# Seven-product groups with their weight sums apart from the instructions that read them, and a fifth such group in five blocks of the first feed-forward

## The chip, the core and the metric

One Trainium2 chip, one of its cores. The metric is the device time of one execution in microseconds (us). The kernel before takes 2227.85 us, the median of three runs (2227.22 to 2228.51).

## What is computed

One decoder layer on 256 tokens of width 2048, all in float32: a SwiGLU feed-forward, two parallel mixers (retention and sliding-window attention), a second SwiGLU feed-forward, and a gated input embedding, each closed by a layer norm. The change lies in the products with weights, above all in the first line below for the first feed-forward:

```
D_MODEL = 2048; SEQ = 256; D_FF = 5632

def swiglu(x, w_gu, w_down):
    g, u = jnp.split(x @ w_gu, 2, axis=-1)
    return (jax.nn.silu(g) * u) @ w_down

h = layer_norm(alpha * h + 0.5 * swiglu(h, w_ffn1_gu[i], w_ffn1_down[i]), ...)
```

## The kernel before, in words

**High and low parts.** TensorE multiplies a rounded format, so each float32 operand is cut into a high part and a low part (the rest). A 128x512 product is then three matmuls: low by high, high by high and high by low (lines 459, 460 and 461, in `Sum.add`). A weight chunk of 128x1024 numbers (512 KB) is loaded by SyncE into a tile whose name begins with `r`; ScalarE casts it to the high part, a tile that begins with `h` (line 107); VectorE subtracts that from the chunk and has the low part, a tile that begins with `l` (line 108). ScalarE and VectorE each work through their instructions strictly in the order in which the program wrote them.

**The first feed-forward's gate and up products** (`f1g` and `f1u` in the profile) run in 11 blocks. A block is 512 gate columns and 512 up columns for all 256 tokens, over 16 slices of 128 of the width, taken in 8 pairs. A pair is two chunks, gate (`0_p`, "a" below) and up (`1_p`, "b"). There are three ways to work a pair p off:
- *Plain* (P): ScalarE casts both chunks, VectorE subtracts both; 24 matmuls of TensorE.
- *Folded* (F): the low part of chunk b is made without VectorE. ScalarE writes the negated high part into the low tile (line 170), GpSimd issues a DMA that adds the raw chunk to it (line 171), and ScalarE later casts the high part (line 187). 24 matmuls.
- *Seven* (S, class `Seven`): the two token halves, the two slices, and the two chunks make a 2x2 by 2x2 product, which is done with seven products in place of eight (Winograd's form): 21 matmuls. For it VectorE forms four sums of raw weights, 128x512 each: t1 and t3 lie in one tile (`uf`), t2 and t4 in another (`vf`); t2 reads t3, and t4 reads t2 (lines 256 to 259). Then come the split of chunk a (`hf`, `lf`), of one quarter, b22 (`bf`), of the tile `uf` (`huf`, `luf`) and of `vf` (`hvf`, `lvf`): four casts on ScalarE, four subtractions on VectorE, 128x1024 but for b22. On the token side the same sums are formed once, in block 0 (`forms_sums`, `seven_forms`, `f1fh` and `f1fl`; lines 533 to 536 and 108), for the pairs 0 to 3.

Block 0 is all plain: 192 matmuls. Blocks 1 to 10 run in the order F F S S F S S P, with pairs 0 to 3 as the four S: 180 matmuls each. The units of a block sum into PSUM banks `f1g` and `f1u`, and the groups of seven share four more banks (`f1NsJ` of block N), which are opened anew for each block.

**The end of a block.** In the last S of a block, the seven products run in another order than in the others, so that the banks shared by the groups are complete early. Then follows `seven_common`: ScalarE copies one bank (`eve`, line 578), and VectorE makes four 128x512 sums (lines 579 to 582). I call these the *fold*. After the plain pair that closes the block, VectorE adds the gate banks (line 1085, twice: *G*), the up banks (line 1085, twice: *U*), ScalarE takes the silu (line 1086), and VectorE multiplies (line 1087: *M*). In the next block, the result is turned for the product with `w_down` by ScalarE copies (lines 219 and 226; tiles `wf1`, `mf1` and `f1a`) and a transposing DMA between them.

**What sets the order.** Weights are prepared ahead of their use by a small planner. `fill` makes the next unit in the plan as long as the prepared ones hold less than 45 matmuls and there is room among the 30 tile slots; each unit carries its number of matmuls as `time` and its number of tiles as `makes` and `keeps`. The half of a folded pair is begun 34 matmuls or more ahead (`FOLD_AHEAD`, `fold_at`). All of this is settled when the program is built. So VectorE's order of work is fixed: splits of the units ahead, with the fold, G, U and M between them at the places where the block's own units were used up.

`Seven` also serves the second feed-forward's gate and up products, both products with `w_down`, and two products of the mixers (`w_in`, `w_ret`).

Of the kernel before, what the change touches and what calls it, by code (L numbers as in the profile page):

```python
# [8 lines left out]
F32 = mybir.dt.float32  # L9
F32R = mybir.dt.float32r  # L10
# [3 lines left out]
ALU = mybir.AluOpType  # L14
PSUM = bass.MemoryType.PSUM

P = 128
# [27 lines left out]

AHEAD = {1: (4, 5), 2: (4,), 3: (4, 5), 4: (4,), 5: (4, 5), 6: (4,), 7: (4, 5), 8: (4,)}
AHEAD_SLOTS = 36

DELAY = {"f1": 2, "f2": 1}

# [14 lines left out]
def layer(ctx: ExitStack, tc: tile.TileContext, io):  # L65
# [16 lines left out]
    def slot(shape, dt, name):  # L82
        return slots.tile(shape, dt, tag="slot", name=name)
# [22 lines left out]
    def split(dst_hi, dst_lo, src, lo_engine=None):  # L106
        act.copy(dst_hi, src)  # L107
        (lo_engine or dve).tensor_tensor(dst_lo, src, dst_hi, ALU.subtract)  # L108
# [124 lines left out]
    class Seven:  # L233
# [12 lines left out]
        def make(self):  # L246
            a, b = self.a, self.b
            nm = a.name
            b11, b21, b12, b22 = a.of(a.raw, 0), a.of(a.raw, 1), b.of(b.raw, 0), b.of(b.raw, 1)
            u, v = (slot([P, 2, 512], F32, w + nm) for w in "uv")  # L250

            def shaped(x):
                return x.rearrange("p (g n) -> p g n", g=2) if a.paired else x

            t1, t3, t2, t4 = (shaped(x) for x in (u[:, 0], u[:, 1], v[:, 0], v[:, 1]))
            dve.tensor_tensor(t1, b11, b12, ALU.add)
            dve.tensor_tensor(t3, b12, b22, ALU.add)  # L257
            dve.tensor_tensor(t2, b11, t3, ALU.add)
            dve.tensor_tensor(t4, t2, b21, ALU.add)  # L259

            def parted(name, x):
                hi, lo = (slot([P, 2, 512], F32R, w + name + nm) for w in "hl")
                split(hi, lo, x)
                return [(hi[:, e], lo[:, e]) for e in range(2)]

            a.make()
            self.b11, self.b21 = a.columns(0), a.columns(1)
            both = slot([P, 2, 512], F32R, "b" + nm)
            self.b22 = both[:, 0], both[:, 1]
            split(shaped(both[:, 0]), shaped(both[:, 1]), b22)  # L270
            self.t1, self.t3 = parted("u", u)
            self.t2, self.t4 = parted("v", v)

    put_by_sums = {}

# [250 lines left out]
    def forms_sums(full):  # L526


        a11, a21 = (full[:, 0::2, t * P : (t + 1) * P] for t in range(2))
        a12, a22 = (full[:, 1::2, t * P : (t + 1) * P] for t in range(2))  # L530
        raw = slot([P, 8, P], F32, "sums")
        f5, f6, f7, f3 = (raw[:, 2 * j : 2 * j + 2, :] for j in range(4))
        dve.tensor_tensor(f5, a21, a22, ALU.subtract)
        dve.tensor_tensor(f7, a11, a21, ALU.subtract)
        dve.tensor_tensor(f6, f5, a11, ALU.subtract)
        dve.tensor_tensor(f3, a12, f6, ALU.add)
        return raw

    def forms_split(raw, hi, lo):

        split(hi, lo, raw)
        return lambda e: [(hi[:, 2 * j + e, :], lo[:, 2 * j + e, :]) for j in range(4)]

    def seven_forms(full, hi, lo, between=None):

# [17 lines left out]
    def units_of(order, sevens, ahead=()):  # L563

        sevens, ahead = list(sevens), list(ahead)
        plain = [p for p in range(KD // 2) if p not in sevens + ahead]
        of = {"S": sevens, "D": ahead, "P": plain, "F": plain}
        return [(kind, of[kind].pop(0)) for kind in order]
# [397 lines left out]
    def gu_units(name, j):  # L966
        if j == 0:
            return [("P", p) for p in range(KD // 2)]
        if name == "f2" and j in AHEAD:
            plain = "P" if j < 4 else "F"  # L970
            return units_of(*((f"P{plain}SDSDSP", SEVEN[:3]) if j % 2 else (f"P{plain}SSDSSP", SEVEN)), AHEAD[j])
        order = "FFSSFSSP" if name == "f1" or j > 8 else "PFSSFSSP"
        return units_of(order, SEVEN[: order.count("S")])

# [28 lines left out]
    def ffn(name, i, ht, norm, keep, residual, keepers, away):  # L1003
# [33 lines left out]
        for j in range(KF // 4):  # L1037
# [22 lines left out]
            def before(u, j=j, offset=KD // 2 - len(units)):  # L1060
                u += offset
                if j == 0 and norm is None and u % 2 == 0:
                    first_chunk(u // 2)
                    if u == 6:
                        slots_for_weights(30)
                    if u == 2:
                        load_constants()
                if j == 0 and u == 7:
                    for g in sorted({p // 2 for p in SEVEN}):
                        hi, lo = (slot([P, 8, P], F32R, f"{name}f{w}{g}") for w in "hl")  # L1070
                        made[g] = seven_forms(keep[g], hi, lo)
# [901 lines left out]
```

## Time and profile before

| what | value |
|---|---|
| median of three runs | 2227.85 us |
| span of the profiled execution | 2226.9 us |
| TensorE busy, matmuls | 2216.5 us, 10137 |
| VectorE busy | 2006.5 us (90%) |
| ScalarE busy | 1440.9 us (65%) |
| TensorE clock granted, mean | 0.999 |
| first feed-forward's gate and up blocks 1 to 10 | from 51.1 to 459.1 us, 40.80 us each |

The answer on the profiled execution gives its span, from the first to the last instruction, and no other time of its own; it is 0.95 us below the median of the runs. An instruction's duration in a timeline includes the tail in which the next one on its engine already starts. What an instruction costs its engine is therefore read as the distance from its start to the start of the next. In a waits list the columns are the total, how often, and the longest. "PEclk" is the granted TensorE clock as a share of full speed.

### The profile page before, as it was taken

To read this page: it belongs to the slowest core of one execution; us is meant where nothing else is said; L and a number is where in the kernel's file an instruction comes from. 1 tells how busy PE (TensorE), PEld (TensorE's weight loads), DVE (VectorE), ACT (ScalarE), POOL (GpSimd) and SP (SyncE) were. 2 spreads that over 40 slices of the span, in tenths; PEclk is the share of its full clock that TensorE was granted. 3 is DMA by queue.
4 is the path that set the end of the run, shared out by engine and by line. 5 is a ranking of instruction groups with operands and counts; after the bars stand their busy time and mean duration, and the time that the engine had idled before them with its cause. 6 is when DMAs were issued, how large, how long until landed. Compare 5 with 4: busy or idle time off the path is not lost.

```text
span 2226.9 us, 29164 instructions
## 1 busy us (share of the span) xinstructions
PE 2216.5 (100%) x10137; PEld 1838.3 (83%) x10137; DVE 2006.5 (90%) x2629; ACT 1440.9 (65%) x1680; POOL 51.7 (2%) x66
## 2 busy tenths in 40 slices
PE   9999999999999999999999999999999999999998
PEld 7888888888888888888788888888888888888887
DVE  6999999999988889789999888779999999999977
ACT  6777777776565545557866567466666677765553
POOL 0000000000000000000000000000000000000000
PEclk9999999999999999999999999999999999999999
DMA  9998998978686889846976568888999988777871
GB/s 310 275 251 251 266 271 233 246 228 256 216 301 239 297 281 336 268 172 228 293 232 236 179 205 319 312 302 270 303 297 298 332 240 270 215 237 240 292 283 68
DMA packets 303917, 576.02 MB, mean 259 GB/s; under 512 B 98829, under 2 KB 103821, under 8 KB 303769
## 3 DMA queue, kind: packets, MB, share of 16 engines
q1 hardware_dynamic: 293576, 541.70, 73.4%
q0 software_dynamic: 8208, 29.89, 7.2%
q10 hardware_dynamic: 1984, 2.58, 0.4%
q8 instruction: 79, 1.29, 0.2%
q14 instruction: 70, 0.57, 0.1%
HBM read 490.20 MB, written 33.55 MB: 235 GB/s over the span
## 4 chain that ended last, share of the span: by engine, by line
PE 94%; DVE 2%; DMA 2%; issue 1%; ACT 0%; SPq 0%; ACTq 0%; DVEq 0%; POOLq 0%
PE f1g L461 3%; PE f1g L459 3%; PE f1g L460 3%; PE rqk L410 3%; PE f1u L461 2%; PE f1u L459 2%; PE f1u L460 2%; PE f2g L461 2%; PE f2g L459 2%; PE f2g L460 2%; PE f2u L461 2%; PE f2u L459 2%; PE f2u L460 2%; PE aqk L410 2%; PE f2e L461 1%; PE f2e L460 1%
## 5 line engine op out<-in xcount | busy, mean ns | idle before, releaser
L108 DVE TENSOR_TENSOR lf_gu<-rf_gu,hf_gu 128x1024 fp32r<-128x1024 f32 (+1 forms) x225 | 268.6, 1210 | 24.9 <-ACT hf_gu L107 24.1
L107 ACT CAST hf_gu<-rf_gu 128x1024 fp32r<-128x1024 f32 (+1 forms) x225 | 229.7, 1039 | 24.7 <-DMA rf_gu<-in_f_gu 24.1
L108 DVE TENSOR_TENSOR lw_in_f<-rw_in_f,hw_in_f 128x1024 fp32r<-128x1024 f32 x140 | 167.9, 1219 | 14.0 <-ACT hw_in_f L107 13.6
L108 DVE TENSOR_TENSOR lf_down<-rf_down,hf_down 128x1024 fp32r<-128x1024 f32 x128 | 153.9, 1220 | 17.3 <-ACT hf_down L107 14.5
L107 ACT CAST hf_down<-rf_down 128x1024 fp32r<-128x1024 f32 x128 | 131.5, 1049 | 41.9 <-DMA rf_down<-in_f_down 15.3
L107 ACT CAST huf_gu<-uf_gu 128x1024 fp32r<-128x1024 f32 x76 | 80.1, 1054 | 113.9 <-DVE uf_gu L257 104.1
L107 ACT CAST hw_in_f<-rw_in_f 128x1024 fp32r<-128x1024 f32 x140 | 140.6, 1048 | 5.9 <-DMA rw_in_f<-in_w_in_f 2.9
L107 ACT CAST hvf_gu<-vf_gu 128x1024 fp32r<-128x1024 f32 x76 | 80.2, 1055 | 32.0 <-DVE vf_gu L259 29.8
L108 DVE TENSOR_TENSOR luf_gu<-uf_gu,huf_gu 128x1024 fp32r<-128x1024 f32 x76 | 92.6, 1218 | 0.0
L108 DVE TENSOR_TENSOR lvf_gu<-vf_gu,hvf_gu 128x1024 fp32r<-128x1024 f32 x76 | 92.6, 1218 | 0.0
L459 PE MATMUL f1g<-hf_gu,xt 128*128 128x512 f32 x232 | 90.6, 390 | 1.5 <-ACT hf_gu L107 1.5
L461 PE MATMUL f1g<-lf_gu,xt 128*128 128x512 f32 x232 | 90.4, 389 | 0.0
L460 PE MATMUL f1g<-hf_gu,xt 128*128 128x512 f32 x232 | 90.3, 389 | 0.0
L459 PE MATMUL f2g<-hf_gu,ht 128*128 128x512 f32 x208 | 81.0, 390 | 0.0
L461 PE MATMUL f2g<-lf_gu,ht 128*128 128x512 f32 x208 | 80.9, 389 | 0.0
L460 PE MATMUL f2g<-hf_gu,ht 128*128 128x512 f32 x208 | 80.9, 389 | 0.0
L459 PE MATMUL f1u<-hf_gu,xt 128*128 128x512 f32 x192 | 74.7, 389 | 0.0
L460 PE MATMUL f1u<-hf_gu,xt 128*128 128x512 f32 x192 | 74.7, 389 | 0.0
L461 PE MATMUL f1u<-lf_gu,xt 128*128 128x512 f32 x192 | 74.7, 389 | 0.0
L171 POOL DMA_DIRECT2D lf_gu<-rf_gu x41 | 35.5, 868 | 1637.7 <-PE f2u L461 989.0
L1086 ACT ACTIVATE eve<-eve 128x1024 f32<-128x1024 f32 x20 | 21.2, 1061 | 74.0 <-DVE eve L1085 74.0
L107 ACT CAST huf_down<-uf_down 128x1024 fp32r<-128x1024 f32 x32 | 33.7, 1052 | 49.7 <-DVE uf_down L257 42.4
(1524 smaller groups left out, 6990.8 us busy)
## 6 DMA issues: line engine op xcount, KB each, us to landing
rf_gu<-in_f_gu SPq DMA_DIRECT2D x362, 512.0 KB
rf_down<-in_f_down SPq DMA_DIRECT2D x176, 512.0 KB
rw_in_f<-in_w_in_f SPq DMA_DIRECT2D x148, 512.0 KB
lf_gu<-rf_gu POOLq DMA_DIRECT2D x41, 512.0 KB, 7.9
rw_rv<-in_w_rv SPq DMA_DIRECT2D x32, 512.0 KB
rw_ret<-in_w_ret SPq DMA_DIRECT2D x32, 512.0 KB
rw_mix<-in_w_mix SPq DMA_DIRECT2D x32, 512.0 KB
rw_pg<-in_w_pg SPq DMA_DIRECT2D x32, 512.0 KB
```

Of the source, the lines that this page charges most:

```text
L107: act.copy(dst_hi, src)
L108: (lo_engine or dve).tensor_tensor(dst_lo, src, dst_hi, ALU.subtract)
L171: pool.dma_start(c.lo, c.raw, accum_op=ALU.add)
L410: pe.matmul(ps[f], hi[:, kk, f * P : (f + 1) * P], rhs(k), start=k == 0, stop=k == n_k - 1,)
L459: pe.matmul(o, al, bh, start=first, stop=False)
L460: pe.matmul(o, ah, bh, start=False, stop=False)
L461: pe.matmul(o, ah, bl, start=False, stop=self.left == 0)
L1086: act.activation(g, g, AF.Silu)
```

## The change

Two things change. First, `Seven.make` is written in another order: t3 is formed ahead of t1, and the subtraction that gives `lf` of chunk a is put between t2 and t4, so that no sum reads the one just before it. The casts on ScalarE keep their order. This holds for all uses of `Seven`. Second, blocks 1, 3, 5, 6 and 8 of the first feed-forward run in the order F S S F S S S P with pair 4 as a fifth S: 177 matmuls in place of 180. For this, block 0 also makes the token-side sums of pair 4 (tile `f1fm`, half the size of the two others). In the program TensorE has 15 rows fewer, GpSimd five fold DMAs fewer. Line numbers shift: line 108 splits are now line 112, 256 to 259 with their splits are 267 to 282, the fold is 591 to 594, G and U are 1102, M is 1104.

```diff
+SEVEN_MORE = 4
+
+FIVE = {"f1": (1, 3, 5, 6, 8), "f2": ()}
...
             t1, t3, t2, t4 = (shaped(x) for x in (u[:, 0], u[:, 1], v[:, 0], v[:, 1]))
-            dve.tensor_tensor(t1, b11, b12, ALU.add)
-            dve.tensor_tensor(t3, b12, b22, ALU.add)
-            dve.tensor_tensor(t2, b11, t3, ALU.add)
-            dve.tensor_tensor(t4, t2, b21, ALU.add)
-
-            def parted(name, x):
-                hi, lo = (slot([P, 2, 512], F32R, w + name + nm) for w in "hl")
-                split(hi, lo, x)
-                return [(hi[:, e], lo[:, e]) for e in range(2)]
-
-            a.make()
-            self.b11, self.b21 = a.columns(0), a.columns(1)
             both = slot([P, 2, 512], F32R, "b" + nm)
             self.b22 = both[:, 0], both[:, 1]
-            split(shaped(both[:, 0]), shaped(both[:, 1]), b22)
-            self.t1, self.t3 = parted("u", u)
-            self.t2, self.t4 = parted("v", v)
+
+            def part(name):
+                hi, lo = (slot([P, 2, 512], F32R, w + name + nm) for w in "hl")
+                return hi, lo, [(hi[:, e], lo[:, e]) for e in range(2)]
+
+            dve.tensor_tensor(t3, b12, b22, ALU.add)
+            dve.tensor_tensor(t1, b11, b12, ALU.add)
+            a.make_hi()
+            self.b11, self.b21 = a.columns(0), a.columns(1)
+            act.copy(a.hi, a.raw)
+            act.copy(shaped(both[:, 0]), b22)
+            dve.tensor_tensor(t2, b11, t3, ALU.add)
+            dve.tensor_tensor(a.lo, a.raw, a.hi, ALU.subtract)
+            dve.tensor_tensor(t4, t2, b21, ALU.add)
+            dve.tensor_tensor(shaped(both[:, 1]), b22, shaped(both[:, 0]), ALU.subtract)
+            uh, ul, (self.t1, self.t3) = part("u")
+            act.copy(uh, u)
+            dve.tensor_tensor(ul, u, uh, ALU.subtract)
+            vh, vl, (self.t2, self.t4) = part("v")
+            act.copy(vh, v)
+            dve.tensor_tensor(vl, v, vh, ALU.subtract)
...
+        n = full.shape[1] // 2
...
-        raw = slot([P, 8, P], F32, "sums")
-        f5, f6, f7, f3 = (raw[:, 2 * j : 2 * j + 2, :] for j in range(4))
+        raw = slot([P, 4 * n, P], F32, "sums")
+        f5, f6, f7, f3 = (raw[:, n * j : n * j + n, :] for j in range(4))
...
+        if j in FIVE[name]:
+            return units_of("FSSFSSSP", SEVEN + (SEVEN_MORE,))
         order = "FFSSFSSP" if name == "f1" or j > 8 else "PFSSFSSP"
...
+                    if name == "f1":
+                        both = slot([P, 2, 4, P], F32R, "f1fm")
+                        made[SEVEN_MORE // 2] = seven_forms(keep[SEVEN_MORE // 2][:, :2], both[:, 0], both[:, 1])
```

**VectorE at the boundary of blocks 2 and 3.** In the names, `f1_gu_3_0_5` is block 3, chunk a (0), pair 5; `f12s` are the shared banks of block 2, `f1g2` and `f1u2` its gate and up banks. Before, from the fold on:

```order
L579 TENSOR_TENSOR evw_1174<-eve_1173,f12s1_865 128x512
L580 TENSOR_TENSOR eve_1173<-evw_1174,f12s2_866 128x512
L581 TENSOR_TENSOR evw_1174<-f12s3_867,evw_1174 128x512
L582 TENSOR_TENSOR evw_1174<-f12s3_867,eve_1173 128x512
L108 TENSOR_TENSOR lf1_gu_3_0_5_1193<-rf1_gu_3_0_5_1138,hf1_gu_3_0_5_1192 128x1024
L1085 TENSOR_TENSOR eve_1173<-eve_1173,f1g20_860 128x512
L1085 TENSOR_TENSOR eve_1173<-eve_1173,f1g21_861 128x512
L1085 TENSOR_TENSOR evw_1174<-evw_1174,f1u20_862 128x512
L1085 TENSOR_TENSOR evw_1174<-evw_1174,f1u21_863 128x512
L1087 TENSOR_TENSOR evw_1174<-eve_1173,evw_1174 128x1024
L256 TENSOR_TENSOR uf1_gu_3_0_0_1243<-rf1_gu_3_0_0_1169,rf1_gu_3_1_0_1171 128x512
```

The fold, the low part of pair 5's chunk a, G, U and M stand here ahead of group 0 of block 3. Now, the fold of block 2 is followed directly by group 0 of block 3, of which these are the last four rows, and then by G, U, M and group 1:

```order
L275 TENSOR_TENSOR vf1_gu_3_0_0_1210<-vf1_gu_3_0_0_1210,rf1_gu_3_0_0_1152 128x512
L276 TENSOR_TENSOR bf1_gu_3_0_0_1211<-rf1_gu_3_1_0_1154,bf1_gu_3_0_0_1211 128x512
L279 TENSOR_TENSOR luf1_gu_3_0_0_1223<-uf1_gu_3_0_0_1209,huf1_gu_3_0_0_1222 128x1024
L282 TENSOR_TENSOR lvf1_gu_3_0_0_1227<-vf1_gu_3_0_0_1210,hvf1_gu_3_0_0_1226 128x1024
L1102 TENSOR_TENSOR eve_1187<-eve_1187,f1g20_877 128x512
L1102 TENSOR_TENSOR eve_1187<-eve_1187,f1g21_878 128x512
L1102 TENSOR_TENSOR evw_1188<-evw_1188,f1u20_879 128x512
L1102 TENSOR_TENSOR evw_1188<-evw_1188,f1u21_880 128x512
L1104 TENSOR_TENSOR evw_1188<-eve_1187,evw_1188 128x1024
L267 TENSOR_TENSOR uf1_gu_3_0_1_1270<-rf1_gu_3_1_1_1185 128x512
```

Block 3 needs its first group one unit earlier, so the group has moved ahead of G, U and M, and M's 128x1024 product now comes one group later.

**VectorE inside one group.** This is group 0 of block 3, before:

```order
L256 TENSOR_TENSOR uf1_gu_3_0_0_1243<-rf1_gu_3_0_0_1169,rf1_gu_3_1_0_1171 128x512
L257 TENSOR_TENSOR uf1_gu_3_0_0_1243<-rf1_gu_3_1_0_1171 128x512
L258 TENSOR_TENSOR vf1_gu_3_0_0_1244<-rf1_gu_3_0_0_1169,uf1_gu_3_0_0_1243 128x512
L259 TENSOR_TENSOR vf1_gu_3_0_0_1244<-vf1_gu_3_0_0_1244,rf1_gu_3_0_0_1169 128x512
L108 TENSOR_TENSOR lf1_gu_3_0_0_1250<-rf1_gu_3_0_0_1169,hf1_gu_3_0_0_1249 128x1024
L108 TENSOR_TENSOR bf1_gu_3_0_0_1253<-rf1_gu_3_1_0_1171,bf1_gu_3_0_0_1253 128x512
L108 TENSOR_TENSOR luf1_gu_3_0_0_1257<-uf1_gu_3_0_0_1243,huf1_gu_3_0_0_1256 128x1024
L108 TENSOR_TENSOR lvf1_gu_3_0_0_1261<-vf1_gu_3_0_0_1244,hvf1_gu_3_0_0_1260 128x1024
```

And now:

```order
L267 TENSOR_TENSOR uf1_gu_3_0_0_1209<-rf1_gu_3_1_0_1154 128x512
L268 TENSOR_TENSOR uf1_gu_3_0_0_1209<-rf1_gu_3_0_0_1152,rf1_gu_3_1_0_1154 128x512
L273 TENSOR_TENSOR vf1_gu_3_0_0_1210<-rf1_gu_3_0_0_1152,uf1_gu_3_0_0_1209 128x512
L274 TENSOR_TENSOR lf1_gu_3_0_0_1215<-rf1_gu_3_0_0_1152,hf1_gu_3_0_0_1214 128x1024
L275 TENSOR_TENSOR vf1_gu_3_0_0_1210<-vf1_gu_3_0_0_1210,rf1_gu_3_0_0_1152 128x512
L276 TENSOR_TENSOR bf1_gu_3_0_0_1211<-rf1_gu_3_1_0_1154,bf1_gu_3_0_0_1211 128x512
L279 TENSOR_TENSOR luf1_gu_3_0_0_1223<-uf1_gu_3_0_0_1209,huf1_gu_3_0_0_1222 128x1024
L282 TENSOR_TENSOR lvf1_gu_3_0_0_1227<-vf1_gu_3_0_0_1210,hvf1_gu_3_0_0_1226 128x1024
```

The 128x1024 `lf` has moved from behind t4 to between t2 and t4; `bf`, `luf` and `lvf` keep their places.

**ScalarE at the end of block 3.** `hvf1_gu_3_0_3` and `hvf1_gu_3_0_4` are the last casts of block 3's last group before and after, and `f1a2` is the turning of block 2's result. Before:

```order
L107 CAST hvf1_gu_3_0_3_1448<-vf1_gu_3_0_3_1432 128x1024
L107 CAST hf1_gu_3_0_7_1466<-rf1_gu_3_0_7_1365 128x1024
L226 COPY f1a2_1470<-mf12_1367 128x2x4x128 x2
L107 CAST hf1_gu_3_1_7_1494<-rf1_gu_3_1_7_1411 128x1024
L107 CAST hf1_gu_4_0_4_1521<-rf1_gu_4_0_4_1452 128x1024
L187 CAST hf1_gu_4_1_4_1525<-rf1_gu_4_1_4_1334 128x1024
L578 COPY eve_1533<-f13s0_1224 128x512
```

And now:

```order
L281 CAST hvf1_gu_3_0_4_1465<-vf1_gu_3_0_4_1449 128x1024
L111 CAST hf1_gu_3_0_7_1492<-rf1_gu_3_0_7_1391 128x1024
L111 CAST hf1_gu_3_1_7_1517<-rf1_gu_3_1_7_1426 128x1024
L230 COPY f1a2_1523<-mf12_1428 128x2x4x128 x2
L111 CAST hf1_gu_4_0_4_1547<-rf1_gu_4_0_4_1469 128x1024
L191 CAST hf1_gu_4_1_4_1551<-rf1_gu_4_1_4_1341 128x1024
L590 COPY eve_1559<-f13s0_1254 128x512
```

Both casts of pair 7 now stand ahead of the two copies to `f1a2`, and the cast of the next block's pair 4, `hf1_gu_4_0_4`, directly behind them. On VectorE the order here is, before, `lvf` of the last group, `lf` of 7a, 7b and 4a, then the fold; now the same, with group 4 as the last group.

3 lines of the change are left out of this document (2 added, 1 removed).

## The prediction

> **What bounds the kernel now.** I read the profile's page first: the span, the engines' busy times, and the chain of work that ended last.
>
> ```profile
> span 2226.9 us, 29164 instructions
> PE 2216.5 (100%) x10137; PEld 1838.3 (83%) x10137; DVE 2006.5 (90%) x2629; ACT 1440.9 (65%) x1680; POOL 51.7 (2%) x66
> PE 94%; DVE 2%; DMA 2%; issue 1%; ACT 0%; SPq 0%; ACTq 0%; DVEq 0%; POOLq 0%
> ```
>
> TensorE (PE) is busy nearly throughout and carries 94% of the chain, but VectorE (DVE) is at 90%. Next comes the table by stretches, for three stretches of the first feed-forward.
>
> ```profile
> core 0: us, PE busy (x) PEld busy (x) DVE busy (x) ACT busy (x) POOL busy (x), PEclk, DMA share, GB/s
> 0.00:51.10 51.10, 48.23 (x211) 40.03 (x212) 32.18 (x39) 31.26 (x35) 2.57 (x8) 1.00 0.96 317
> 91.90:132.70 40.80, 40.80 (x181) 33.78 (x180) 38.59 (x47) 30.41 (x34) 2.60 (x3) 1.00 0.95 251
> 132.70:173.50 40.80, 40.80 (x181) 33.78 (x180) 38.60 (x47) 30.62 (x34) 2.59 (x3) 1.00 0.95 258
> ```
>
> The last two rows are blocks 2 and 3. TensorE has no gap in them, at a granted clock of 1.00, and a block of 180 matmuls takes 40.80 us, so one matmul costs **0.2267 us**. VectorE is busy for 38.60 of the 40.80. That is the number to keep in mind: the change takes matmuls from the engine at 100% and gives work to one that has 2.2 us per block. The waits of TensorE over the whole span confirm that there is little else to win:
>
> ```profile
> PE f1g L459 <- ACT hf_gu L107: 1.5, 1, 1.5
> PE f2u L461 <- DMA lf_gu<-rf_gu: 0.8, 1, 0.8
> PE mr1a L461 <- DVE lw_ret L108: 0.5, 1, 0.5
> ```
>
> **VectorE's own ledger.** Its timeline at the end of block 2 and in the first group of block 3, with TensorE's first matmul of block 3 behind it:
>
> ```profile
> 125.94 0.69 DVE L579 TENSOR_TENSOR evw<-eve,f12s 128x512 f32<-128x512 f32 x1
> ...
> 128.66 1.22 DVE L108 TENSOR_TENSOR lf_gu<-rf_gu,hf_gu 128x1024 fp32r<-128x1024 f32 x1
> 129.79 1.28 DVE L1085 TENSOR_TENSOR eve<-eve,f1g 128x512 f32<-128x512 f32 x2
> 132.23 1.37 DVE L1085 TENSOR_TENSOR evw<-evw,f1u 128x512 f32<-128x512 f32 x2 [1.16 <-PE f1u L461]
> 133.70 1.23 DVE L1087 TENSOR_TENSOR evw<-eve,evw 128x1024 f32<-128x1024 f32 x1
> 134.84 0.69 DVE L256 TENSOR_TENSOR uf_gu<-rf_gu,rf_gu 128x512 f32<-128x512 f32 x1
> 135.44 0.69 DVE L257 TENSOR_TENSOR uf_gu<-rf_gu 128x512 f32<-128x512 f32 x1
> 136.17 0.69 DVE L258 TENSOR_TENSOR vf_gu<-rf_gu,uf_gu 128x512 f32<-128x512 f32 x1
> 136.89 0.69 DVE L259 TENSOR_TENSOR vf_gu<-vf_gu,rf_gu 128x512 f32<-128x512 f32 x1
> 137.50 1.22 DVE L108 TENSOR_TENSOR lf_gu<-rf_gu,hf_gu 128x1024 fp32r<-128x1024 f32 x1
> 138.64 0.69 DVE L108 TENSOR_TENSOR bf_gu<-rf_gu,bf_gu 128x512 fp32r<-128x512 f32 x1
> 139.24 1.22 DVE L108 TENSOR_TENSOR luf_gu<-uf_gu,huf_gu 128x1024 fp32r<-128x1024 f32 x1
> 140.38 1.22 DVE L108 TENSOR_TENSOR lvf_gu<-vf_gu,hvf_gu 128x1024 fp32r<-128x1024 f32 x1
> 141.51 0.68 DVE L256 TENSOR_TENSOR uf_gu<-rf_gu,rf_gu 128x512 f32<-128x512 f32 x1
> ```
> ```profile
> 132.71 0.39 PE L459 MATMUL f1g<-hf_gu,xt 128*128 128x512 f32 x1
> ```
>
> Start to start: a 128x512 sum costs 0.60 us where it does not read the one before it (134.84 to 135.44), and 0.73 and 0.72 where it does. A 128x1024 subtraction costs 1.14. A group costs 6.67 (134.84 to 141.51). The fold costs 2.72 (125.94 to 128.66), G 1.20, U 1.47, M 1.14. The fold's end at 128.66 lies **4.05 us ahead** of the block's start at 132.71. I call this lead the state of VectorE: f = -4.05. It cannot grow, since U waits 1.16 us for TensorE in each block.
>
> Now the last group of block 3 and what follows it, on VectorE and on ScalarE (ACT):
>
> ```profile
> 156.04 0.68 DVE L256 TENSOR_TENSOR uf_gu<-rf_gu,rf_gu 128x512 f32<-128x512 f32 x1
> ...
> 158.15 0.69 DVE L259 TENSOR_TENSOR vf_gu<-vf_gu,rf_gu 128x512 f32<-128x512 f32 x1
> ...
> 164.35 2.36 DVE L108 TENSOR_TENSOR lf_gu<-rf_gu,hf_gu 128x1024 fp32r<-128x1024 f32 x2 [0.37 <-ACT hf_gu L107]
> 166.73 0.69 DVE L579 TENSOR_TENSOR evw<-eve,f13s 128x512 f32<-128x512 f32 x1
> ```
> ```profile
> 158.93 1.05 ACT L107 CAST hvf_gu<-vf_gu 128x1024 fp32r<-128x1024 f32 x1 [0.46 <-DVE vf_gu L259]
> 159.88 1.05 ACT L107 CAST hf_gu<-rf_gu 128x1024 fp32r<-128x1024 f32 x1
> 160.83 2.58 ACT L226 COPY f1a<-mf 128x1024 uint16<-128x1024 uint16 x2
> 163.28 1.99 ACT L107 CAST hf_gu<-rf_gu 128x1024 fp32r<-128x1024 f32 x2
> 165.17 1.04 ACT L187 CAST hf_gu<-rf_gu 128x1024 fp32r<-128x1024 f32 x1
> 166.12 0.58 ACT L578 COPY eve<-f13s 128x512 f32<-128x512 f32 x1
> ```
>
> The reader is to see that VectorE does not set its own pace here. ScalarE cannot cast `vf` until t4 ends (158.15 + 0.69 = 158.84). From there it works without a gap through one cast, one more, two copies, three casts and the copy `eve`, which ends at 166.70; the fold starts at 166.73, **7.89 us after the end of t4**. The fold's end, 169.45, is 13.4 us after the group's start.
>
> **The change part by part.**
>
> *Fifteen matmuls fewer* (three in each of five blocks): 15 x 0.2267 = **-3.4 us**. All of it lies on the chain.
>
> *The order inside a group.* Now all five 128x512 operations may go at 0.60, and three 128x1024 at 1.14: 3.00 + 3.41 = 6.41, 0.26 less than now. But t4 now stands behind t3, t1, t2 and `lf`. It starts 3 x 0.60 + 1.14 = 2.94 after the group's start and ends at 3.62, where it ended at 2.80 (158.84 less 156.04). Everything that ScalarE has queued behind `hvf` moves with it: the casts of pair 7, the two copies, the casts of the next block's chunks, `eve`. So the fold starts at 3.62 + 7.89 = 11.5 after the start of the last group and ends at **14.2**, 0.8 later than now, whatever VectorE saves in that group. That eats most of the four times 0.26 that a block gains. A fifth-S block has the same instructions between t4 and `eve` in another order, and gives the same 14.2.
>
> The Trainium skill, page "VectorE: DVE Perf Modes", section "The DRAIN you can't avoid", says that the next operation waits until the pipe is empty, with or without semaphores, and points to a later section for operations that wait for nothing; by its rule the reordering is worth nothing, and the sum would be that of the third rival. The trace here disagrees, with 0.60 against 0.73.
>
> *The fifth group on VectorE.* Count from the fold's end to the `lvf` of the fifth group, the last tile that this group needs: five groups 32.05, G, U and M 3.81, one `lf` 1.14, together **37.0 us**. On TensorE the fifth group begins after 24 + 21 + 21 + 24 + 21 + 21 = 132 matmuls, and its ninth matmul reads `lvf`: 140 x 0.2267 = 31.7 after the block's start. Without a stall, the fold must have ended at f = 31.7 - 37.0 = **-5.3**. Today's -4.05 is already too late, so the block stalls by f + 5.3.
>
> What f is: a block of four S, in VectorE's time from one fold's end to the next, takes `lf`, G, U, M (4.95), two groups, `lf`, one group (20.4), and 14.2, in all 39.5, against 40.8 on TensorE. It wins back 1.3. A block of five S has 30.6 up to its last group (37.0 less one group) and then 14.2, in all 44.8, against 40.1 plus its stall s: f becomes f + 4.7 - s, and with s = f + 5.3 that is -0.6, always. Hence:
> - blocks 3, 5 and 8, each behind a block of four S that stands behind one of five: f = -0.6 - 1.3 = -1.9, stall **3.4** each, 10.2 (0.9 of it at the second group, ready at -1.9 + 16.6 = 14.7 and read at 61 x 0.2267 = 13.8, the rest at the fifth);
> - block 6, directly behind block 5: f = -0.6, stall **4.7**;
> - block 1: in block 0 VectorE now makes a third set of token-side sums. The trace has the two others:
>
> ```profile
> 42.37 0.42 DVE L533 TENSOR_TENSOR sums<-xraw 128x256 f32<-128x256 f32 x1
> ...
> 46.26 0.42 DVE L533 TENSOR_TENSOR sums<-xraw 128x256 f32<-128x256 f32 x1
> ...
> 50.14 1.22 DVE L108 TENSOR_TENSOR lf_gu<-rf_gu,hf_gu 128x1024 fp32r<-128x1024 f32 x1
> ```
>
> One takes 3.88. For one of half the size I bound it by nothing and 3.88, and take half, 1.9, as its tiles are half as wide: the first group starts at 52.1. It must be followed by 34.4 us (five groups, 1.20 of sums of block 0, one `lf`) before 51.1 + 31.7 = 82.8: stall **3.7**, with 1.8 and 5.7 as ends.
>
> The blocks of four S do not stall: from f = -0.6 their last `lvf` is ready at 31.1, and the 144th matmul reads it at 32.4. The five fold DMAs that go had cost TensorE nothing, since its list of waits has none on them in this stage. ScalarE's casts for the fifth group (three and a half in place of three for a folded pair) lie within the 10 us per block in which it is idle.
>
> *Elsewhere* the new order serves the groups of the other stages. Their TensorE hardly waits today (the 0.8 and 0.5 above), so I take 0, between -1.4 and +1.5.
>
> **Sum**: -3.4 + 3.7 + 10.2 + 4.7 = +15.2. Against the profiled execution, whose span of 2226.9 lies 0.95 under the median, that is 2242.1 in span; against the median of 2227.85 it is **2243.0 us**. If each stall is wrong by 20%, the time is between 2239 and 2247.
>
> **The rivals.**
>
> *ScalarE does not delay the fold* (the copies or casts move into one of its idle spells, of which it has 10 us per block). Then the fold follows VectorE: 6.41 + 3 x 1.14 + 2.72 = 12.5 in place of 14.2. A block of five S ends at f = -2.3, one of four S wins back 3.0, so f = -5.3: blocks 3, 5 and 8 do not stall, block 6 stalls by 3.0, block 1 by 3.7. Sum +3.3, **2231 us**. For it: the waits on ScalarE are short today, 0.37 in the row above. Against it: the gapless ScalarE rows between 158.93 and 166.70. Chance 0.15.
>
> *No stall at all: the tiles are ready in time.* This ends on the other side, at -3.4: **2224.4 us**, which is within 0.2%, or 2223 and below if the 1.3 us of waits by `f2u` and `mr1a` go too. It decides at f = -5.3 in every fifth-S block, and the fold could end there at the earliest: the first two shared banks are complete 36 matmuls, some 8.0 us, before the next block, plus 2.72. For block 6 that needs, beyond a ScalarE that never delays, a group of 5.8 us in place of 6.41. For it: VectorE's busy time includes tails that overlap, so that 38.60 overstates its load by some us. Against it: all pitches above are start to start already. Chance 0.18, of it 0.08 for under 2223.4.
>
> *The reordering saves VectorE nothing* (a group stays at 6.67, as with a pipe that always empties). Then a block of four S wins back 0.5, the five S need f = -6.6 and leave -0.9, and stalls are 5.2 three times, 5.7 and 5.0: 26.3 - 3.4 gives **2250.8 us**. Against it: 0.60 between the independent sums of today. Chance 0.04.
>
> *The clock falls after a stall.* If TensorE's clock were halved for the 13 matmuls of the group that follow each stall, 13 x 0.2267 = 2.9 more in five blocks: **2258 us**. Against it: the first stretch above has TensorE not busy for 2.9 us, and the granted clock reads 1.00. Chance 0.06.
>
> The Trainium skill, page "TensorE: Matmul & The Clock Gate", part "The HAM clock gate", has the clock fall to half after an idle window of about 3.4 us. The pieces of the stalls above are shorter than that, so by the page the clock stays, and so far the trace, at 1.00 after the first stretch, agrees.
>
> That the change does not do what it says is no rival: the program has 15 matmul rows fewer, and the sums stand apart.
>
> **How the numbers follow.** The forecast has 0.57, the rivals 0.15, 0.18, 0.04 and 0.06. 0.2% is 4.5 us, about what a measurement of this kernel can tell from no change: faster means under 2223.4, slower over 2232.3. Faster: 0.08. Same: 0.10 of the no-stall case and half of the first rival, 0.18. Slower: the rest, 0.74. The range runs from 2225, so that most of the no-stall case is left out below, to 2252, so that the clock case is left out above.
>
> **What would show it.** In the changed kernel, TensorE's waits name VectorE's `luf` and `lvf` (lines 279 and 282) in blocks 1, 3, 5, 6 and 8, some 3 to 5 us each; these blocks last 43 to 45 us, the others 40.8, and the gate and up products end near 474.5 in place of 459.1. VectorE's wait for `hf` of pair 7 or of the next pair 4 grows to 1.4 to 1.6 us per block. A group takes 6.4. I am wrong if fifth-S blocks last near 40.1: then either ScalarE did not hold the fold, or a fold ended 5.3 us ahead of its block.

## The result, and the profile after

The changed kernel takes **2242.09 us** (2241.16 to 2243.70, four runs) against 2227.66 us for the kernel before in the same comparison: **1.0069 times as long, 95% interval 1.0057 to 1.0082**, or 14.4 us more. The forecast was 2243.0. The profiled execution has a span of 2239.1 in place of 2226.9. From its page:

```profile
span 2239.1 us, 29151 instructions
PE 2222.3 (99%) x10122; PEld 1837.1 (82%) x10122; DVE 2011.3 (90%) x2669; ACT 1443.2 (64%) x1686; POOL 47.4 (2%) x61
PE 81%; DVE 3%; ACT 1%; issue 1%; DMA 1%; ACTq 0%; SPq 0%; DVEq 0%; POOLq 0%
```

Fifteen matmuls fewer, and TensorE's busy time is 5.8 us *longer*, since a matmul's duration grows where it is held up or where the clock is low. Its share of the chain fell from 94% to 81%. The table by stretches, for blocks 2 to 5 and then 6 and 8, with the columns of the table in the prediction:

```profile
93.06:133.86 40.80, 40.80 (x181) 33.79 (x180) 39.05 (x50) 30.86 (x34) 2.58 (x3) 1.00 0.91 238
133.86:178.67 44.81, 42.98 (x179) 33.89 (x177) 42.97 (x53) 30.73 (x34) 1.75 (x2) 0.96 0.84 241
178.67:219.47 40.80, 40.80 (x182) 33.79 (x180) 39.04 (x49) 31.13 (x34) 2.58 (x3) 1.00 0.86 235
219.47:263.46 43.99, 42.44 (x178) 34.14 (x177) 42.16 (x53) 31.21 (x34) 1.72 (x2) 0.96 0.86 246
263.46:308.15 44.69, 42.96 (x178) 33.89 (x177) 42.86 (x53) 30.46 (x33) 1.75 (x2) 0.96 0.79 228
348.95:391.15 42.20, 40.76 (x179) 33.07 (x177) 40.33 (x49) 30.51 (x33) 1.72 (x2) 1.00 0.84 254
```

Blocks of four S last 40.80 as before. Blocks of five last 42.98 (block 1, from 50.08 to 93.06), 44.81, 43.99, 44.69 and 42.20, where 177 matmuls need 40.13. I call the difference the excess: 2.85, 4.68, 3.86, 4.56, 2.07, together **18.0 us** (forecast: 18.6). The ten blocks end at 472.75 and last 422.67 in place of 408.0: **+14.7**. The spans differ by 12.2, since block 1 begins 1.0 earlier and the rest of the span is 1.5 shorter; the profiled execution took 2241.18 us, 0.9 under the median. The granted clock, the column behind the engines, is 0.96 in three of the five.

VectorE's timeline at the end of block 2 follows. 117.47 is the start of the last group, line 275 is its t4, line 591 begins the fold, and the last row, the next group's first sum, marks the fold's end; some rows between are left out:

```profile
117.47 0.68 DVE L267 TENSOR_TENSOR uf_gu<-rf_gu 128x512 f32<-128x512 f32 x1
118.07 0.68 DVE L268 TENSOR_TENSOR uf_gu<-rf_gu,rf_gu 128x512 f32<-128x512 f32 x1
...
120.41 0.68 DVE L275 TENSOR_TENSOR vf_gu<-vf_gu,rf_gu 128x512 f32<-128x512 f32 x1
...
123.89 1.22 DVE L112 TENSOR_TENSOR lf_gu<-rf_gu,hf_gu 128x1024 fp32r<-128x1024 f32 x1
126.59 2.36 DVE L112 TENSOR_TENSOR lf_gu<-rf_gu,hf_gu 128x1024 fp32r<-128x1024 f32 x2 [1.49 <-ACT hf_gu L111]
128.97 0.69 DVE L591 TENSOR_TENSOR evw<-eve,f12s 128x512 f32<-128x512 f32 x1
...
131.69 0.68 DVE L267 TENSOR_TENSOR uf_gu<-rf_gu 128x512 f32<-128x512 f32 x1
```

The group takes 6.42 (117.47 to 123.89), as summed. The wait for ScalarE has grown from 0.37 to 1.49. The fold ends at 131.69, 14.22 us after the group's start, and 2.17 ahead of block 3 (133.86).

### The profile page after: what moved, and what is told of

Same layout as the page of the kernel before. It is cut to its first block, busy times and chain, and to the rows that moved or that the text cites. A ratio compares the mean times of both kernels' runs of the same rounds, so it can differ in the third digit from the quotient of the medians.

```text
span 2239.1 us, 29151 instructions
## 1 busy us (share of the span) xinstructions
PE 2222.3 (99%) x10122; PEld 1837.1 (82%) x10122; DVE 2011.3 (90%) x2669; ACT 1443.2 (64%) x1686; POOL 47.4 (2%) x61
## 4 chain that ended last, share of the span: by engine, by line
PE 81%; DVE 3%; ACT 1%; issue 1%; DMA 1%; ACTq 0%; SPq 0%; DVEq 0%; POOLq 0%
PE rqk L420 3%; PE f2g L469 2%; PE f2g L470 2%; PE f2g L471 2%; PE f2u L471 2%; PE f2u L469 2%; PE f2u L470 2%; PE aqk L420 2%; PE f2e L469 1%; PE f1d L470 1%; PE f1e L469 1%; PE f2d L470 1%; PE f1d L469 1%; PE f2d L469 1%; PE f2e L470 1%; PE f1e L471 1%
## 5 line engine op out<-in xcount | busy, mean ns | idle before, releaser
L112 DVE TENSOR_TENSOR lf_gu<-rf_gu,hf_gu 128x1024 fp32r<-128x1024 f32 (+1 forms) x144 | 169.9, 1204 | 47.9 <-ACT hf_gu L111 47.0
L112 DVE TENSOR_TENSOR lw_in_f<-rw_in_f,hw_in_f 128x1024 fp32r<-128x1024 f32 x132 | 158.0, 1218 | 14.0 <-ACT hw_in_f L111 13.9
L111 ACT CAST hf_gu<-rf_gu 128x1024 fp32r<-128x1024 f32 (+1 forms) x144 | 145.0, 1035 | 16.1 <-DMA rf_gu<-in_f_gu 15.9
L112 DVE TENSOR_TENSOR lf_down<-rf_down,hf_down 128x1024 fp32r<-128x1024 f32 x96 | 115.1, 1219 | 23.2 <-ACT hf_down L111 19.7
L111 ACT CAST hf_down<-rf_down 128x1024 fp32r<-128x1024 f32 x96 | 98.5, 1049 | 27.5 <-DMA rf_down<-in_f_down 13.9
L274 DVE TENSOR_TENSOR lf_gu<-rf_gu,hf_gu 128x1024 fp32r<-128x1024 f32 x81 | 98.5, 1217 | 0.5
L469 PE MATMUL f1g<-hf_gu,xt 128*128 128x512 f32 x217 | 85.4, 394 | 0.5 <-ACT hf_gu L111 0.4
L271 ACT CAST hf_gu<-rf_gu 128x1024 fp32r<-128x1024 f32 x81 | 84.5, 1043 | 1.4 <-DMA rf_gu<-in_f_gu 1.4
L470 PE MATMUL f1g<-hf_gu,xt 128*128 128x512 f32 x217 | 85.1, 392 | 0.0
L471 PE MATMUL f1u<-lf_gu,xt 128*128 128x512 f32 x172 | 66.9, 389 | 0.0
L470 PE MATMUL f1u<-hf_gu,xt 128*128 128x512 f32 x172 | 66.9, 389 | 0.0
L469 PE MATMUL f1u<-hf_gu,xt 128*128 128x512 f32 x172 | 66.9, 389 | 0.0
```

What stands on the lines that cost most here:

```text
L271: act.copy(a.hi, a.raw)
L274: dve.tensor_tensor(a.lo, a.raw, a.hi, ALU.subtract)
L469: pe.matmul(o, al, bh, start=first, stop=False)
L470: pe.matmul(o, ah, bh, start=False, stop=False)
L471: pe.matmul(o, ah, bl, start=False, stop=self.left == 0)
```

## The experiments

"Before" is the kernel before, run on the same chip in the same comparison. f is the fold's end less the next block's start, as in the prediction.

### Only the new order

```diff
-FIVE = {"f1": (1, 3, 5, 6, 8), "f2": ()}
+FIVE = {"f1": (), "f2": ()}
```

Block 0 then makes no third set of token-side sums either.

> Only the new order inside a group; all blocks keep four groups of seven. Theory (the fifth group on VectorE and ScalarE costs the time, the order alone is neutral): blocks of 40.80 us, no stall of TensorE in the first feed-forward, 2227.7 us within 1.5. The fold still ends 14.2 us after the last group's start, but four groups win back 1.3 per block. Rival (the late t4 is what costs): the ScalarE-bound fold end alone stalls TensorE, several us over 2227.7.

2228.14 us against 2226.14, 1.0009 (1.0000 to 1.0018). The gate and up blocks in one row, and VectorE's waits in them:

```profile
49.79:457.79 408.00, 408.00 (x1801) 337.98 (x1800) 381.21 (x462) 305.34 (x333) 24.17 (x28) 1.00 0.94 259
```
```profile
DVE lf_gu L112 <- ACT hf_gu L111: 14.9, 10, 1.5
DVE evw L1102 <- PE f1u L471: 9.2, 8, 1.2
```

The first wait was 4.9 us in the same blocks before. Forty groups that are each 0.25 shorter save VectorE 10 us, and its wait for ScalarE grows by just these 10. The fold still ends 4.05 ahead of the block. In these blocks the order by itself gives TensorE nothing and takes nothing from it. The 2.0 us between the medians, at the edge of the interval, do not come from this stage.

### Only the fifth group

The lines of `make` are those of before; `FIVE` is as in the change.

> Only the fifth group in the five blocks, with the old order inside a group (6.67 us, t4 ending 2.8 us after the group's start, fold end 13.4 after the last group's start). Theory: a block of five must have the fold 6.6 us ahead, and leaves f = -1.7; a block of four wins back 1.3; stalls 5.0 + 3 x 3.6 + 4.9 = 20.7, less 3.4: 2245 us, 2 to 3 us slower than the change as a whole. Rival (the late t4 is what costs): faster than the change as a whole, near 2230.

2245.08 us against 2226.14, 1.0085 (1.0071 to 1.0099): 18.9 over before, with gate and up blocks of 426.4 us in place of the change's 422.7. So the reordering does help once there is a fifth group, by 3.7 us in this stage where 2 to 3 were expected, and the late t4 alone is not the loss.

### Copies behind the fold

```diff
-            later(DELAY[name] + 3, joined)
+            later(DELAY[name] + (7 if name == "f1" and j < 9 else 3), joined)
```

> The change as it is, but in the first feed-forward the two ScalarE copies that end a block's turning come four steps later, behind the fold's copy instead of ahead of the casts that the fold waits for. Theory (ScalarE's queue behind t4 sets the fold's end): fold end 12.5 in place of 14.2 us after the last group's start, blocks 3, 5 and 8 nearly without stall, 2.7 to 3 us left in blocks 1 and 6: 2230.5 us (2229 to 2233). Rival (VectorE's own load is the limit): no change, 2242.

2242.23 us against 2226.14, 1.0073 (1.0059 to 1.0087). **My expectation failed.** The fold does end 12.55 after the last group's start, without a wait, but f reaches only -3.7 ahead of a block of five, where I had -5.3, and in block 6 the excess is 6.6. VectorE's waits in the gate and up blocks tell why:

```profile
DVE lf_gu L274 <- ACT hf_gu L271: 7.8, 5, 1.8
DVE lf_gu L112 <- ACT hf_gu L111: 3.2, 2, 1.7
```

The waits for the casts of the single chunks fell from 13.9 to 3.2, and a new one of 1.8 stands at line 274, where a group behind the copies' new place needs its first cast. ScalarE's 2.4 us of copies had only been put in front of other work that VectorE waits for. The gate and up blocks are 1.6 us shorter than the change's (421.1), which the medians do not show.

### Copies on GpSimd

```diff
-                turn.join(raws[-1])
+                turn.join(raws[-1], pool.tensor_copy if name == "f1" and j < 9 else act.copy)
```

`join` now takes the instruction that copies as its second argument.

> The change as it is, but the two copies that end a block's turning are done by GpSimd, which is idle, and no longer by ScalarE. Theory (ScalarE's queue holds the fold, and moving the copies behind the fold only made new waits in the next block's first groups): fold end 12.5 us after the last group's start, no new waits, a block of four wins back 2.9 us, blocks 3, 5 and 8 nearly without stall, 3 us each left in blocks 1 and 6: 2.8 us over the kernel before. Rival 1 (VectorE's own load is the limit): 14 to 16 over, as the change. Rival 2 (GpSimd's copies slow VectorE's instructions beside them): VectorE's subtractions longer than 1.14 start to start, and no gain.

2233.05 us against 2226.78, 1.0031 (1.0019 to 1.0042): 6.3 over before, 8 less than the change. Blocks 3 and 4, and block 6:

```profile
134.15:174.77 40.62, 40.45 (x179) 33.07 (x178) 40.27 (x51) 27.13 (x31) 12.65 (x4) 1.00 0.86 255
174.77:215.57 40.80, 40.80 (x182) 33.78 (x181) 40.26 (x50) 29.75 (x33) 14.34 (x5) 1.00 0.89 249
256.19:301.06 44.87, 43.06 (x179) 34.01 (x178) 43.25 (x54) 29.76 (x33) 12.60 (x4) 0.96 0.90 255
```

Blocks 3, 5 and 8 have an excess of 0.49 each, f is -5.2 ahead of them, and VectorE's wait for the casts is 1.5 us in all. What is left is block 1 (3.4) and block 6 behind block 5 (4.7, of which 1.6 is the clock). This is the first rival of the prediction made real, at 6.3 in place of 3.3: 0.5 us remain where I had none, and block 6 lost to the clock. GpSimd needs 5.7 us in the mean for a copy that took ScalarE 1.3, and VectorE did not feel it (its subtractions are compared in the last section):

```profile
L230 POOL COPY f1a<-mf 128x1024 uint16<-128x1024 uint16 x18 | 102.2, 5723 | 2.2 <-PE f1u L471 1.9
L230 POOL COPY f1a<-mf x18: 1347/4558/10982, 79.4 to 416.2; 128x1024 uint16<-128x1024 uint16 x18
```

The second row has the shortest, the median and the longest, in ns. The mean hides two kinds: the first copy of each pair takes 7.7 to 11.0 us, the second 1.35 to 1.37.

### t4 earlier

```diff
-            dve.tensor_tensor(a.lo, a.raw, a.hi, ALU.subtract)
+            dve.tensor_tensor(shaped(both[:, 1]), b22, shaped(both[:, 0]), ALU.subtract)
             dve.tensor_tensor(t4, t2, b21, ALU.add)
-            dve.tensor_tensor(shaped(both[:, 1]), b22, shaped(both[:, 0]), ALU.subtract)
+            dve.tensor_tensor(a.lo, a.raw, a.hi, ALU.subtract)
```

The cast of b22 also goes ahead of that of chunk a on ScalarE.

> The change as it is, but with the short subtraction of b22 between t2 and t4, and the long one of chunk a behind t4 (its cast behind that of b22 on ScalarE). t4 ends 3.1 us after the group's start in place of 3.6, with the group still at 6.4. Theory (ScalarE's queue behind t4 sets the fold's end): fold end 13.65 in place of 14.2; stalls of 3.0, 3 x 2.3 and 4.15 in place of 3.7, 3 x 3.4 and 4.7: 4.6 us faster than the change. Rival (VectorE's load is the limit): as the change.

2237.89 us against 2226.78, 1.0050 (1.0037 to 1.0063): 11.1 over, 3.3 less than the change. 4.6 were expected. The gate and up blocks last 419.4, 3.2 less than the change's, at a granted clock of 1.00 in all five blocks of five. VectorE in block 3's last group: its first sum, t4, a subtraction with the wait for ScalarE, and the instruction behind the fold, whose start is the fold's end:

```profile
161.92 0.68 DVE L267 TENSOR_TENSOR uf_gu<-rf_gu 128x512 f32<-128x512 f32 x1
...
164.33 0.68 DVE L275 TENSOR_TENSOR vf_gu<-vf_gu,rf_gu 128x512 f32<-128x512 f32 x1
...
171.46 1.23 DVE L112 TENSOR_TENSOR lf_gu<-rf_gu,hf_gu 128x1024 fp32r<-128x1024 f32 x1 [0.77 <-ACT hf_gu L111]
...
175.61 1.22 DVE L112 TENSOR_TENSOR lf_gu<-rf_gu,hf_gu 128x1024 fp32r<-128x1024 f32 x1
```

t4 ends 3.1 after the group's start and the fold 13.69, as expected. The excess of blocks 3, 5, 6 and 8 is 2.2, 2.2, 4.1 and 2.2, also as expected; block 1 has 4.0 in place of 3.0. Half a microsecond of t4 in each block is worth 3.2 us in all: the same instructions, in another order.

### One subtraction less for VectorE

```diff
-            return units_of("FSSFSSSP", SEVEN + (SEVEN_MORE,))
+            return units_of("FSSFSSSF", SEVEN + (SEVEN_MORE,))
```

> The change as it is, but with the last pair of the five blocks folded in place of plain: one 128x1024 subtraction, 1.14 us, less for VectorE in each, with ScalarE's order behind t4 unchanged. Theory (ScalarE's queue behind t4 sets the fold's end): fold end still 14.2 us after the last group's start, and the time as the change's, 14 to 16 us over the kernel before. Rival (VectorE's load is the limit): up to 5 x 1.14 = 5.7 us faster than the change, 9 over.

2242.71 us against 2226.34, 1.0075 (1.0063 to 1.0088): as the change. VectorE's wait in the gate and up blocks:

```profile
DVE lf_gu L112 <- ACT hf_gu L111: 19.6, 10, 2.5
```

In the change it is 13.9 there. The fold still ends 14.2 us after the last group's start, and the gate and up blocks last 422.9 (change: 422.7). The 5.7 us that VectorE was spared, five times 1.14, came back as 5.7 us of waiting. With the run on GpSimd this settles that ScalarE's queue behind t4, and not VectorE's load, ends the cycle.

### The idle time filled

```diff
+                if len(sevens) == 5 and p == sevens[-1] and at < 2:
+                    for _ in range((2, 8)[at]):
+                        pe.matmul(q2.ap[:16], zero_r, u.t1[0], start=False, stop=False)
                 to.add(left, right)
```

Left out here: `at` counts the products of the group, and `zero_r` is a tile of 16 columns of zeros, made once at the start.

> The change as it is, but with ten matmuls of zeros in the last group of each block of five (two ahead of its first product, eight ahead of its second), in the place where TensorE stood still, so that its clock should stay at 1.00. They add exact zeros and 2.3 us of matmuls per block. Theory (VectorE and ScalarE set the length of a pair of blocks; what the slow clock costs is given back by a smaller stall in the next block): same as the change, 2242 within 1.5. Rival (the clock's loss of some 4.9 us in blocks 3, 5 and 6 comes on top of the stalls): 2237.

2261.32 us against 2226.14, 1.0159 (1.0145 to 1.0173). Not what either theory had, by a mistake of mine: the condition also holds in eight blocks of the second feed-forward, where nothing was idle, and 80 matmuls there cost 80 x 0.2267 = 18.1. Repeated with the condition on the first feed-forward:

> The ten matmuls of zeros again, now in the first feed-forward's five blocks alone (the run before had them in eight blocks of the second feed-forward too, 80 x 0.2267 = 18.1 us). They add exact zeros and 2.3 us of matmuls per block. Theory (VectorE and ScalarE set the length of a pair of blocks, what the slow clock costs is given back by a smaller stall in the next block): the gate and up blocks as long in all as in the change, 422.7 us within 1, and the time the change's within 1.5, 16 us over the kernel before in this comparison. Rival (the clock's loss of 4.9 us in blocks 3, 5 and 6 comes on top): 5 us less than the change.

2244.29 us against 2226.78, 1.0079 (1.0067 to 1.0092). Blocks 3, 5 and 6, and then blocks 1 to 10 in one row:

```profile
135.73:179.38 43.65, 43.23 (x188) 33.94 (x187) 41.79 (x51) 30.60 (x34) 1.75 (x2) 1.00 0.82 245
220.18:263.63 43.45, 43.27 (x189) 33.86 (x187) 41.60 (x52) 30.24 (x34) 1.72 (x2) 1.00 0.85 246
263.63:308.75 45.12, 43.48 (x188) 33.85 (x187) 43.25 (x53) 31.55 (x34) 1.76 (x2) 1.00 0.80 223
50.17:474.73 424.56, 420.63 (x1837) 338.35 (x1835) 405.87 (x497) 311.45 (x340) 20.79 (x24) 1.00 0.86 243
```

The clock stays at 1.00 in each, and the gate and up blocks last 424.6 us: not 4.9 less than in the change (422.7), as the rival has it, but 1.9 more, 0.9 beyond what the theory allowed. VectorE shows where these come from. Its first group of block 1 starts at 51.50 in this trace and at 49.80 in that of the change, 1.7 later. From there to the end of block 9's fold it takes 380.1 us here, with the clock at 1.00, and 379.9 us in the change, where the clock fell three times. In the run before this one, which has the same ten matmuls in these blocks, it takes 380.1 from a start at 50.31, and the blocks last 423.3. So in the change the clock's loss did not come on top.

### Three fifth groups

```diff
-FIVE = {"f1": (1, 3, 5, 6, 8), "f2": ()}
+FIVE = {"f1": (3, 6, 9), "f2": ()}
```

> The change with a fifth group in blocks 3, 6 and 9 alone. Theory (a block of five leaves the fold 0.6 us ahead, each block of four wins back 1.3, the stall is f + 5.3): stalls of 1.2, 2.1 and 2.1, less 2.0 for nine matmuls: 3.4 us over the kernel before. Rival (each fifth group costs the same, whatever stands ahead of it): three fifths of the change's 14.4 to 16, so 8.6 to 9.6 over.

2237.27 us against 2226.78, 1.0045 (1.0032 to 1.0059): 10.5 over, near the rival's number and far from mine. The three blocks of five:

```profile
131.39:175.01 43.62, 41.58 (x178) 32.83 (x177) 41.76 (x51) 30.78 (x34) 1.73 (x2) 1.00 0.84 245
256.61:298.93 42.32, 40.77 (x179) 32.99 (x177) 40.48 (x50) 30.48 (x33) 1.72 (x2) 1.00 0.88 252
380.53:424.40 43.87, 42.34 (x178) 34.17 (x177) 42.03 (x53) 30.52 (x34) 1.72 (x2) 0.96 0.82 242
```

Excess 3.49, 2.19 and 3.74. The state f, read from the trace ahead of blocks 2 to 10, is -0.82, -2.16 (block 3), -0.84, -2.18, -3.48 (block 6), -0.88, -2.21, -3.54 (block 9), -2.48: a block of five leaves about -0.85, a block of four wins back 1.3, and the stall follows f, so a fifth group's price does depend on what stands ahead of it. Two things went wrong in my number. Block 3 starts from -2.16, not from -4.05, because the third set of sums in block 0 leaves block 1 late. And in block 9 the clock fell, for 1.6 us that nothing gave back. That makes 7.6 us in the gate and up blocks. In the profiled execution, which took 2237.43 us, there is also a wait for a DMA of 2.1 us in the second feed-forward, with slow matmuls behind it, which this edit does not touch. Two of the five runs had a granted clock of 0.999 and 1.000 and took 2235.83 and 2235.57, which is still 8.8 over the kernel before at least. What makes up the rest over the 7.6 stays open.

### The pieces put together

Copies on GpSimd, the last pair folded, and fifth groups in blocks 3, 5, 7 and 9:

```diff
-FIVE = {"f1": (1, 3, 5, 6, 8), "f2": ()}
+FIVE = {"f1": (3, 5, 7, 9), "f2": ()}
```

> Copies on GpSimd, the fifth group in blocks 3, 5, 7 and 9 alone (none in block 1 with its late start, none directly behind another), and in these blocks the last pair folded in place of plain, which takes one 128x1024 subtraction from VectorE. Theory: the fold ends 5.2 us ahead of each block of five (TensorE sets that limit), a stall of 0.5 us is left in each, against 0.7 us of matmuls saved: 0.8 us under the kernel before, which is no difference to be measured. VectorE's pair of blocks, 42.0 + 37.9, then fits into TensorE's 80.9. Rival (the stalls come from a fifth group however it is fed): 2 to 4 us per block over.

2227.02 us against 2226.34, 1.0004 (0.9995 to 1.0013): no difference. Blocks 3 and 5:

```profile
131.69:172.31 40.62, 40.44 (x179) 33.07 (x177) 40.24 (x50) 28.09 (x32) 12.19 (x5) 1.00 0.92 270
213.11:253.75 40.64, 40.47 (x179) 33.07 (x177) 40.28 (x50) 28.12 (x32) 12.04 (x5) 1.00 0.92 265
```

The stalls are gone but for 0.5 us each, and with them the loss. The folded last pair has little part in it. VectorE in block 3, the two subtractions ahead of the fold and the fold's first instruction:

```profile
163.65 3.46 DVE L112 TENSOR_TENSOR lf_gu<-rf_gu,hf_gu 128x1024 fp32r<-128x1024 f32 x2
167.03 0.67 DVE L591 TENSOR_TENSOR evw<-eve,f13s 128x512 f32<-128x512 f32 x1
L112 DVE TENSOR_TENSOR lf_gu<-rf_gu,hf_gu x41: 1212/1217/2240, 52.8 to 449.5; 128x1024 fp32r<-128x1024 f32 x41
```

Two subtractions should take 2.28 from start to start, and take 3.38. In each of the four blocks the second of them lasts 2.2 us where 1.2 is usual (the last row has the shortest, the median and the longest, in ns), and it ends 1.0 us after a GpSimd copy beside it. So the 1.14 us that the folded pair spares VectorE are lost again, and the fold ends 12.5 us after the last group's start, as in the run with the copies alone, and not 11.4. But 0.5 of the 0.68 us that a fifth group saves is still paid, and no version here beats the kernel before.

## Why the prediction was right, point by point

**The fifteen matmuls, -3.4.** Right: 177 matmuls in place of 180, at the same pitch.

**The group at 6.41 and the fold at 14.2.** Right: 6.42 and 14.2, in blocks 1 to 9 (behind block 10, where another stage begins, the fold ends after 16.4). What the reordered group saves VectorE, it hands to its wait for ScalarE (first experiment).

**The stall as f + 5.3, the state after a block of five, and the 1.3 won back.** Right as a mechanism. Where the clock held (blocks 1 and 8), a block of five left f = -0.83 and -0.88, for a forecast of -0.6; blocks of four won back 1.34. The constant was a little small: in blocks 3, 5, 6 and 8 `lvf` of the fifth group is read 3.41, 2.12, 3.05 and 1.90 late, at f = -2.17, -3.41, -2.50 and -3.64, which is f + 5.5 in all four.

**Block 1, +3.7.** Mis-sized: 2.85. I took the third set of sums at 1.9 us, starting where the second had ended; it took 2.4, but the two before it ended sooner than in the kernel before, and the first group started at 49.80, 0.3 ahead of the block instead of 1.0 behind its start. With that start my own sum gives a stall of 2.4, and most of the 0.4 above it is the same small constant.

**Blocks 3, 5, 8 at 3.4 and block 6 at 4.7.** The sum of 14.9 came out as 15.2, but not in these pieces: 4.68, 3.86, 2.07 and, in block 6, 4.56. That the sum fits is in part luck: a slow clock adds to one block and shortens the stall of the next, and the forecast had neither. The step that failed is the sentence that the clock stays. TensorE in the last group of block 3:

```profile
165.48 0.50 PE L471 MATMUL f13s<-lf_gu,xt 128*128 128x512 f32 x1 [0.22 <-DVE lf_gu L274]
...
166.05 0.39 PE L470 MATMUL f13s<-huf_gu,f1fm 128*128 128x512 f32 x1
167.82 0.53 PE L471 MATMUL f13s<-luf_gu,f1fm 128*128 128x512 f32 x1 [1.38 <-DVE luf_gu L279]
168.15 0.62 PE L469 MATMUL f13s<-hvf_gu,f1fm 128*128 128x512 f32 x1
168.57 0.63 PE L470 MATMUL f13s<-hvf_gu,f1fm 128*128 128x512 f32 x1
169.00 0.74 PE L471 MATMUL f13s<-lvf_gu,f1fm 128*128 128x512 f32 x1
...
171.63 0.40 PE L471 MATMUL f1g<-lf_gu,xt 128*128 128x512 f32 x1
171.86 0.39 PE L469 MATMUL f1u<-bf_gu,f1fm 128*128 128x512 f32 x1
```

The matmul at 167.82 starts 1.77 us after the one before it, 1.5 more than at full speed. After this stall matmuls start 0.43 apart in place of 0.23, for some 3.5 us. `lvf` is read at 169.00, 3.4 after its due time of 133.86 + 31.7, as forecast; the slow matmuls behind it add 1.2 (1.6 in block 5, 1.4 in block 6). This is the rival *the clock falls*, to which I gave 0.06, with the price wrong. It fell in three of five blocks, in the profiled execution, and it did not add to the sum: VectorE and ScalarE work on while TensorE is slow, so block 3 left f = -2.07 and not -0.83, block 4 brought it to -3.41, and block 5's stall at `lvf` was 2.1 in place of 3.4. The length of a pair of blocks is set by VectorE and ScalarE; what TensorE loses in one block it gets back as a shorter wait in the next. The runs with the idle time filled show it: with the clock at 1.00, VectorE needs the same 380 us from its first group to block 9's fold. Only a loss with no block of five behind it is not given back, as in the run with three fifth groups.

**Elsewhere, 0.** From the end of the gate and up blocks to the end, the span has 1766.3 us in place of 1767.8: 1.5 less, just past the -1.4 that I had allowed.

**The closeness of the sum.** It is in part luck. The sum was worked out for the profiled execution, whose span it puts at 2242.1; the span is 2239.1. Of the 3.0 us between them, 0.6 lie in the stalls, 1.0 in the earlier start of block 1 and 1.5 in the rest of the span. The median of the runs, 0.9 under the forecast, is nearer than that.

**The signs.** The blocks of five last 42.2 to 44.8 us for 43 to 45, the others 40.8, and the gate and up products end at 472.75 for 474.5. The waits are shorter than I had them, 3 to 5 us by `luf` and `lvf`. In block 3 they are these, and the other blocks of five differ little:

```profile
PE f13s L471 <- DVE luf_gu L279: 1.4, 1, 1.4
PE f13s L471 <- DVE lf_gu L274: 0.4, 2, 0.2
PEld f13s L471 <- DVE lvf_gu L282: 0.5, 1, 0.5
```

The rest of the excess lies in matmuls beside these waits that start more than 0.2267 apart, and in the low clock.

**The rivals.** *ScalarE does not delay the fold* was built with GpSimd's help and is worth 8 of the 14.4 us. *The reordering saves nothing* is excluded by the 0.60 us from 117.47 to 118.07 and the 6.42 of the group. *No stall at all* does not occur with a fifth group at any place tried; the nearest is 0.5 us.

## What to carry to other kernels

When two engines alternate, sum each one's cycle from one point at which they meet to the next, in start-to-start times, and include the in-order queue of any third engine between them: here one 128x512 sum delayed eight ScalarE instructions behind it, and 0.5 us of its place was worth more than 1.14 us of VectorE's load. Work taken from the engine that seems full turns into waiting if another queue ends the cycle, and a stall elsewhere in the cycle is given back if the bottleneck works on meanwhile. Moving the copies within ScalarE's queue chose, for the most part, who waits; moving them to an idle engine did help, although that engine and VectorE held each other up in places.

## What the runs showed of the hardware

In the change TensorE's clock fell after idle pieces of some 1.5 us at most, in block 3 one of 0.4 and one of 1.5 within 2.8 us; matmuls then started 0.43 us apart for about 3.5 us. In block 8, with a piece of 1.4 us, it stayed at full speed, and so it did in block 1 with 0.4 and 1.5. In the run with three fifth groups it stayed in block 3, with 0.4 and 1.5, and fell in block 9, with one of 1.5. So the length of these pieces alone does not decide it. What decides was not settled. The Trainium skill, page "TensorE: Matmul & The Clock Gate", part "The HAM clock gate", has the clock at half after an idle window of about 3.4 us, with windows that run freely. The trace agrees on the half speed and the length of the slow stretch; it disagrees on the idle time needed, since TensorE had executed matmuls in every stretch of 3.4 us.

The Trainium skill, page "GPSIMD Engine Reference", section "Specifications", says that GpSimd's memory interfaces are shared with VectorE and contend with its instructions that have two inputs in SBUF. The traces agree, and they show who pays. In the run with the copies on GpSimd alone it is GpSimd. Its nine short copies, 1.35 to 1.37 us, lie beside the fold, whose instructions (lines 591 to 594) read one input from PSUM. The nine long ones, 7.7 to 11.0 us, begin beside a group, whose instructions read both inputs from SBUF, and each ends 1.2 to 1.3 us after the last of VectorE's subtractions ahead of the fold, about the length of a short copy. VectorE's subtractions show no cost there: between 100 and 460 us, line 279 has a mean of 1217 ns in that run and in the changed kernel. In the run with the pieces together VectorE pays too, 1.0 us in each block of five. That the two engines hold each other up is read from these times; no run changed it alone.
